# The second layer's input projection by one level of Strassen products, with values, gates and head outputs kept with tokens on partitions

## The chip, the cores and the metric

The kernel runs on one core of one Trainium2 chip. The metric is the device time of one execution in microseconds: the median of the runs, 807.87 us over three runs (806.84 to 807.95) for the kernel before. A profiled execution gives a trace of each engine: PE multiplies matrices, DVE (VectorE), ACT (ScalarE) and POOL (GpSimd) work on elements, SP issues most of the DMAs.

## The reference

Two pre-norm layers over 512 tokens of width 1024, then a last RMSNorm. Layer 1 (attention and pooling) stays as it is. Layer 2 is bidirectional retention with four heads; what the change touches is its input projection `h @ w_in`, whose columns are q, k (256 each for a head), v and gate (512 each for a head):

```python
def retention_layer(x, cos_r, sin_r, norm_g, w_in, decay_fwd, decay_bwd, gn_g, w_out):
    h = rms_norm(x, norm_g)
    q, k, v, gate = jnp.split(h @ w_in, [RET_QK, 2 * RET_QK, 2 * RET_QK + RET_V], axis=-1)
    q = apply_rope(q.reshape(B_, T, RET_HEADS, RET_DK), cos_r, sin_r)
    k = apply_rope(k.reshape(B_, T, RET_HEADS, RET_DK), cos_r, sin_r) * (RET_DK ** -0.5)
    o = retention(q, k, v)          # scores q k^T times a decay in |i - j|, times v, both directions
    o = group_norm(o) * gn_g        # over the 512 channels of a head
    return (o * jax.nn.silu(gate)) @ w_out
```

## The kernel before

Every fp32 product is made of three matmuls: each operand is split into a high part that PE takes whole and a remainder, and `mm3` (L71) issues high x high (L72), and the two mixed products (L75, L76). The split of a weight block of 128x1024 is `wsplit`: the high part is a cast on ACT (L108), the remainder a subtraction on DVE (L109); that of an activation is `split` (L81 on ACT, L82 on DVE). All work is handed to a tile framework that orders the instructions of each engine by itself as the program is built; only what `pin` names is held in program order. Each engine then runs its own list strictly in order, and waits for others by semaphores. SBUF tiles come from pools by tag (`BUFS`, L46), PSUM tiles from three tags: `mm` 4, `sc` 2, `tr` 2 banks.

In layer 2, x lies with channels on partitions (`xT`, eight chunks of 128 channels x 512 tokens). `close_layer` (L651) adds the last quarter of layer 1's output to a chunk (L652), scales it by the norm's gain and splits it (L655 on ACT, L656 on DVE). The token factor of the norm, r2, comes from Squares (L835), sums (L836), `token_sums` (L177), a power on POOL (L174, `pow_mhalf`) and `bcast` (L191), which spreads it over the partitions; it is applied behind the products, to the rope tables (L843, L844), the values (L714) and the gates (L743).

For each head the program computes q and k with channels on partitions (`qk_gemm`, four `gemm_T` blocks of 24 matmuls), rope (`rope_pair`, L690), the output projection of the head before (`r_out`, L770, 96 matmuls into the residual `acc`, which holds tokens on partitions), the decay table (`decay`, L660), the values with tokens on partitions (`r_values`, L700, 96 matmuls), the scores (`r_scores`, L724), the gates with channels on partitions (`r_gates`, L738, 96 matmuls), and the head's output with channels on partitions (`r_head_out`, L751). The residual is turned by 32 transposes (`acc_in`, L672) and copied out of PSUM on ACT (L682). After the last head, `finish` (L795) and `scale_out` (L814) do the last norm.

Of the kernel before, what the change touches and what calls it, by code (L numbers as in the profile page):

```python
# [12 lines left out]
F32R = mybir.dt.float32r  # L13
# [24 lines left out]
def trunk(ctx: ExitStack, tc: tile.TileContext, x, positions, a_norm_g, a_w_in, a_q_norm_g, a_w_uq,  # L38
# [7 lines left out]
    BUFS = {"hT": 16, "xT": 8, "y": 8, "V": 8, "qk": 8, "pt": 8, "t": 9, "l1": 13,   # L46
            "raw": 3, "wH": 4, "wL": 3, "sm": 24}
    PBUFS = {"mm": 4, "sc": 2, "tr": 2}

    def S(tag, shape=(P, T), dt=F32):  # L50
        count[0] += 1
        return sb.tile(list(shape), dt, tag=tag, name=f"{tag}_{count[0]}", bufs=BUFS[tag])

# [225 lines left out]
    posf = C("posf", (P, T))  # L279
# [123 lines left out]
    WB = 576  # L403
    plu = {}

    def pool_in(gi):
# [5 lines left out]
        def pool_ev(m, pt):  # L412
            u = S("pt", (P, WB))[:, :W]
# [4 lines left out]
            while step < w:  # L418
                nx = S("pt", (P, WB))[:, :W]
# [222 lines left out]
    idi = S("raw", (P, 1024), I32)[:, :E]  # L642
# [5 lines left out]
    h2H, h2L = [None] * 8, [None] * 8  # L648
    sqs = S("l1")

    def close_layer(m, pt):  # L651
        V.tensor_add(xT[m], pt, xT[m])  # L652
        h = S("hT", dt=F32R)
        l = S("hT", dt=F32R)
        act(h, xT[m], AF.Copy, scale=col(RN + m))  # L655
        V.scalar_tensor_tensor(out=l, in0=xT[m], scalar=col(RN + m), in1=f(h), op0=ALU.mult, op1=ALU.subtract)  # L656
        h2H[m], h2L[m] = h, l
# [9 lines left out]

    wr = r_w_in[0]
    wo = r_w_out[0]
    acc = [[None] * 2 for _ in range(4)]  # L670

    def acc_in(hf):  # L672
        pts = [PS(tag) for tag in ("tr", "tr", "sc", "sc")]
        for t in range(4):
            for k in range(4):
                nc.tensor.transpose(pts[t][:, k * P:(k + 1) * P], xT[hf * 4 + k][:, t * P:(t + 1) * P], ident)
        return pts

    def acc_set(hf, pts):
        for t in range(4):  # L680
            a = S("xT")
            nc.scalar.copy(a, pts[t])  # L682
            acc[t][hf] = a

    def qk_gemm(c0, n=2):
        pts = []
        gemm_T(wr, c0, n, lambda m, pt: pts.append(pt), h2H, h2L)
        return pts

    def rope_pair(pts):  # L690
        a, b, c, d = S("t"), S("t"), S("t"), S("t")
        V.tensor_mul(a, pts[0], cosr)
        V.tensor_mul(c, pts[0], sinr)
        V.tensor_mul(b, pts[1], sinr)
        V.tensor_mul(d, pts[1], cosr)
        V.tensor_sub(a, a, b)
        V.tensor_add(c, c, d)
        return split(a, "qk"), split(c, "qk")

    def r_values(h):  # L700
        pts = [PS("mm") for _ in range(4)]
        for kp in range(4):
            uH, uL = wunit(wr[kp * 256:(kp + 1) * 256, 2048 + h * T:2048 + (h + 1) * T]
                           .rearrange("(k p) n -> p k n", p=P), 2, T)
            for k2 in range(2):
                k = kp * 2 + k2
                for t in range(4):
                    tk = slice(t * P, (t + 1) * P)
                    mm3(pts[t], h2H[k][:, tk], h2L[k][:, tk], uH[:, k2], uL[:, k2], k == 0, k == 7)
        vH, vL = [], []  # L710
        for t in range(4):
            v = S("t")
            sm = S("sm", (P, 4))
            act(v, pts[t], AF.Copy, scale=r2[:, t:t + 1], accum_out=sm[:, 0:1])  # L714
# [5 lines left out]
            vH.append(hh)  # L720
            vL.append(ll)
        return vH, vL

    def r_scores(q, k, ds):  # L724
        sH, sL = [], []
        for j in range(4):
# [6 lines left out]
            a, b = split(s, "pt")  # L733
            sH.append(a)
            sL.append(b)
        return sH, sL

    def r_gates(h, m0=0, n=4):  # L738
        gs = []

        def ev(m, pt):
            t = S("t")
            V.tensor_mul(t, pt, R)  # L743
            g = S("l1")
            act(g, t, AF.Silu)
            gs.append(g)

        gemm_T(wr, 4096 + h * T + m0 * P, n, ev, h2H, h2L)
        return gs

    def r_head_out(h, vv, ss, gs, ytag):  # L751
        ys = []
        sq = None
        for m in range(4):
            ms = slice(m * P, (m + 1) * P)
            pt = PS("mm")
            for j in range(4):
                mm3(pt, vv[0][j][:, ms], vv[1][j][:, ms], ss[0][j], ss[1][j], j == 0, j == 3)
            t = S("t")
            act(t, pt, AF.Square)  # L760
            if sq is None:
                sq = t
            else:
                V.tensor_add(sq, sq, t)
            y = S("t")
            V.scalar_tensor_tensor(out=y, in0=pt, scalar=col(GN + h * 4 + m), in1=gs[m], op0=ALU.mult, op1=ALU.mult)
            ys.append(split(y, ytag))
        return ys, sq

    def r_out(h, ys, rs, last=False, mid=None):  # L770
        for hf in range(2):
            us = [wunit(wo[h * T + i * 256:h * T + (i + 1) * 256, hf * T:(hf + 1) * T]
                        .rearrange("(k p) n -> p k n", p=P), 2, T) for i in range(2)]
            for t in range(4):
                tk = slice(t * P, (t + 1) * P)
                n = 2 if last and hf == 1 and t == 3 else 1
                for c in range(n):
# [5 lines left out]
                    if mid and hf == 0 and t == 0:  # L783
# [42 lines left out]

    pend = None
    for h in range(4):
        if h == 0:
            pts = acc_in(0)  # L830
            pq = qk_gemm(0, 1)
            act(sqs, xT[0], AF.Square)
            for m in range(1, 8):
                t = S("t")
# [79 lines left out]
```

## Time and profile before

| | |
|---|---|
| median of three runs | 807.87 us (806.84 to 807.95) |
| the profiled execution | 807.98 us |
| its span (first to last instruction) | 806.2 us |
| mean granted PE clock | 0.997 |
| PE busy, DVE busy, ACT busy, POOL busy | 99%, 65%, 45%, 2% |

In the page and in the views of the trace, a row names the line of the kernel, the engine, the operation and its tiles, out<-in. A timeline row begins with the start in us from the span's start and the duration; a bracket behind a row is the engine's idle time before it and who released it. A window row gives the stretch, its length, and each engine's busy time with its count of instructions.

### The profile page before, as it was taken

The page shows a single profiled execution, that of the slowest core. Times are in us where ns is not written, and L with a number is a line of the kernel's source. Part 1 is how long each engine was busy: PE and PEld are TensorE (multiplying, and loading weights), DVE is VectorE, ACT ScalarE, POOL GpSimd, SP SyncE. Part 2 cuts the span into 40 slices and gives each one's busy share as a digit, 9 for nine tenths or more (in the row PEclk, how much of TensorE's full clock was granted, in tenths as well). Part 3 has the DMA queues.
Part 4 walks back from the last instruction along what each step waited for, and adds up shares of the span by engine and source line. Part 5 has one row for each costly group of instructions (what it writes and reads, how often), then busy time and mean ns, then how long its engine had stood idle before and what let it go on. Part 6 is the DMA issues. An engine that isn't in the chain of part 4 may idle for free.

```text
span 806.2 us, 9481 instructions
## 1 busy us (share of the span) xinstructions
PE 796.5 (99%) x3590; PEld 656.1 (81%) x3590; DVE 524.1 (65%) x895; ACT 364.4 (45%) x595; POOL 18.9 (2%) x45
## 2 busy tenths in 40 slices
PE   8999999999999999999999999999999999999996
PEld 6888888888888888888888888888888888888885
DVE  4689976767748687899564648363483535753655
ACT  6645346676627734328254522263232543253222
POOL 0010000000000000000000000000000000000003
PEclk9999999999999999999999999999999999999999
DMA  7523233221222212233323113323123221232112
GB/s 224 150 75 90 85 82 75 54 80 62 72 81 80 79 53 78 79 101 111 103 79 105 52 53 105 98 59 105 53 68 115 79 78 53 85 99 78 53 53 104
DMA packets 93589, 68.30 MB, mean 85 GB/s; under 512 B 7484, under 2 KB 83304, under 8 KB 93544
## 3 DMA queue, kind: packets, MB, share of 16 engines
q1 hardware_dynamic: 93240, 67.18, 28.4%
q8 instruction: 28, 0.46, 0.3%
q10 hardware_dynamic: 304, 0.53, 0.2%
q14 instruction: 17, 0.14, 0.1%
HBM read 64.29 MB, written 2.10 MB: 82 GB/s over the span
## 4 chain that ended last, share of the span: by engine, by line
PE 97%; DMA 1%; POOL 1%; issue 0%; SPq 0%; ACT 0%; DVE 0%; POOLq 0%
PE mm L72 29%; PE mm L75 29%; PE mm L76 29%; PE sc L72 2%; PE sc L76 2%; PE sc L75 2%; PE tr L560 2%; PE sc L541 1%; PE sc L542 1%; DMA l<-in_x_dram 1%; POOL t L820 0%; POOL sm L816 0%; PE tr L182 0%; PE mm L345 0%; PE mm L344 0%
## 5 line engine op out<-in xcount | busy, mean ns | idle before, releaser
L108 ACT CAST wH<-raw 128x1024 fp32r<-128x1024 f32 (+3 forms) x133 | 125.4, 946 | 291.2 <-PE mm L75 137.4
L109 DVE TENSOR_TENSOR wL<-raw,wH 128x1024 fp32r<-128x1024 f32 (+3 forms) x133 | 144.5, 1090 | 94.5 <-PE mm L76 42.1
L72 PE MATMUL mm<-hT,wH 128*128 128x512 f32 x480 | 187.9, 391 | 0.0
L75 PE MATMUL mm<-hT,wH 128*128 128x512 f32 x480 | 187.6, 391 | 0.0
L76 PE MATMUL mm<-hT,wL 128*128 128x512 f32 x480 | 187.6, 391 | 0.0
L76 PEld LDWEIGHTS mm<-hT,wL 128*128 128x128 f32 x480 | 90.6, 189 | 18.9
L75 PEld LDWEIGHTS mm<-hT,wH 128*128 128x128 f32 x480 | 90.4, 188 | 18.7
L72 PEld LDWEIGHTS mm<-hT,wH 128*128 128x128 f32 x480 | 90.5, 189 | 18.5
L75 PE MATMUL mm<-wL,hT 128*128 128x512 f32 (+1 forms) x164 | 63.0, 384 | 0.0
L72 PE MATMUL mm<-wH,hT 128*128 128x512 f32 (+1 forms) x164 | 62.9, 384 | 0.0
L76 PE MATMUL mm<-wH,hT 128*128 128x512 f32 (+1 forms) x164 | 62.8, 384 | 0.0
L786 DVE SCALAR_TENSOR_TENSOR xT<-mm,sm,xT 128x512 f32<-128x512 f32 (+1 forms) x33 | 24.2, 732 | 23.8 <-PE mm L76 23.8
L743 DVE TENSOR_TENSOR t<-mm,R 128x512 f32<-128x512 f32 x16 | 11.1, 691 | 43.2 <-PE mm L76 43.2
L75 PE MATMUL mm<-pt,V 128*128 128x512 f32 x96 | 37.8, 393 | 0.0
L72 PE MATMUL mm<-pt,V 128*128 128x512 f32 x96 | 37.5, 391 | 0.0
L76 PE MATMUL mm<-pt,V 128*128 128x512 f32 x96 | 37.5, 390 | 0.0
L75 PE MATMUL mm<-wL,y 128*128 128x512 f32 x96 | 37.4, 389 | 0.0
L72 PE MATMUL mm<-wH,y 128*128 128x512 f32 x96 | 37.4, 389 | 0.0
L76 PE MATMUL mm<-wH,y 128*128 128x512 f32 x96 | 37.3, 389 | 0.0
L75 PE MATMUL mm<-y,wH 128*128 128x512 f32 x96 | 37.2, 389 | 0.0
L76 PE MATMUL mm<-y,wL 128*128 128x512 f32 x96 | 37.2, 389 | 0.0
L72 PE MATMUL mm<-y,wH 128*128 128x512 f32 x96 | 37.2, 390 | 0.0
(238 smaller groups left out, 1329.8 us busy)
## 6 DMA issues: line engine op xcount, KB each, us to landing
raw<-in_r_w_in_dram SPq DMA_DIRECT2D x48, 512.0 KB, 3.8
raw<-in_a_w_in_dram SPq DMA_DIRECT2D x25, 512.0 KB, 3.9
raw<-in_a_w_out_dram SPq DMA_DIRECT2D x16, 512.0 KB, 3.5
raw<-in_r_w_out_dram SPq DMA_DIRECT2D x16, 512.0 KB, 3.4
l<-in_x_dram SPq DMA_DIRECT2D x8, 256.0 KB, 5.6
out_dram<-t SPq DMA_DIRECT2D x8, 256.0 KB, 2.0
raw<-in_a_w_in_dram SPq DMA_DIRECT2D x4, 384.0 KB, 4.1
raw<-in_a_w_uq_dram SPq DMA_DIRECT2D x8, 192.0 KB, 2.4
```

The source lines that it names most:

```text
L72: i = mm(pt, lhsT=lH, rhs=rH, start=st, stop=False)
L75: mm(pt, lhsT=lH, rhs=rL, start=False, stop=False)
L76: mm(pt, lhsT=lL, rhs=rH, start=False, stop=sp)
L108: then(nc.scalar.copy(h[:, c], raw[:, c]))
L109: then(V.tensor_sub(l[:, c], raw[:, c], f(h[:, c])))
L541: mm(pt, lhsT=st[:, tk], rhs=KH, start=False, stop=False)
L542: mm(pt, lhsT=st[:, tk], rhs=KL, start=False, stop=True)
L560: nc.tensor.transpose(pt[:, t * P:(t + 1) * P], es[t][:, j * P:(j + 1) * P], ident)
L743: V.tensor_mul(t, pt, R)
L786: V.scalar_tensor_tensor(out=a, in0=pt[:, :T // n], scalar=rs[:, t:t + 1], in1=a, op0=ALU.mult, op1=ALU.add)
```

## The change

The input projection of layer 2 is a 2x2 block product: the contraction is cut into even and odd 128-channel chunks, the tokens into two halves of 256, and the columns into two blocks, q and k of a head in `qk(h)`, gates and values of a head in `vg(h)`. `strassen` computes it with seven block products instead of eight (the form of Winograd): the activation forms A11, A12, A22, S1 to S4 are made once, at the end of layer 1, by `left_forms` on DVE and split (ACT, DVE); the weight sums are made for each head by POOL (`minus`), 12 of 128x1024 a head, and all weight blocks and sums are split as before. The parts of the result are gathered from three sets of PSUM banks (X, Y, Z) by `read`. In `qk` the 256 tokens of a half are the moving operand; in `vg` they are the stationary one, and 512 weight columns move.

Values, gates and head outputs now all have tokens on partitions. So the gate takes r2 as a per-partition scale of its Silu, the squares for the group norm are ACT's accumulators, and `turn` transposes the gated output back before `r_out`. Those accumulators replace `token_sums`; for r2 the Squares are taken of the turned residual (`residual`). The rope tables times R are kept as two pairs, CS and SC, one pair for each half of the tokens. The tiles that had tags of their own share one class of 72 buffers of 2 KB; `raw` has 6 buffers instead of 3, `tw` is new.

```diff
-    BUFS = {"hT": 16, "xT": 8, "y": 8, "V": 8, "qk": 8, "pt": 8, "t": 9, "l1": 13, 
-            "raw": 3, "wH": 4, "wL": 3, "sm": 24}
+    BUFS = {"b": 72, "raw": 6, "tw": 4, "wH": 4, "wL": 3, "sm": 24}
...
+    def left_forms(out, e, o, ge, go):
...
+        for src, g, a, b in ((e, ge, raw["A11"], a21), (o, go, raw["A12"], raw["A22"])):
+            V.tensor_scalar(out=a, in0=src[:, :H2], scalar1=g, scalar2=1.0, op0=ALU.mult, op1=ALU.mult)
+            V.tensor_scalar(out=b, in0=src[:, H2:], scalar1=g, scalar2=1.0, op0=ALU.mult, op1=ALU.mult)
+        V.tensor_add(raw["S1"], a21, raw["A22"])
+        V.tensor_sub(raw["S2"], raw["S1"], raw["A11"])
+        V.tensor_sub(raw["S3"], raw["A11"], a21)
+        V.tensor_sub(raw["S4"], raw["A12"], raw["S2"])
+        for z, names in ((z1, ("A11", "A12")), (z2, ("A22", "S1")), (z3, ("S2", "S3")), (z4, ("S4",))):
+            n = H2 * len(names)
+            h, l = S("hT", dt=F32R), S("hT", dt=F32R)
+            nc.scalar.copy(h[:, :n], z[:, :n])
+            V.tensor_sub(l[:, :n], z[:, :n], f(h[:, :n]))
...
+    def strassen(load, chunks, run, read):
...
+        product("A11", "X", b11, True)
+        t1 = [minus(b12[i], b11[i]) for i in rng]
+        product("S1", "Z", t1, True)
+        t2 = [minus(b22[i], t1[i]) for i in rng]
+        product("S2", "Y", t2, True)
+        b21 = [load(1, 0, i) for i in rng]
+        product("A12", "X", b21, False)
+        t4 = [minus(b21[i], t2[i]) for i in rng]
+        product("S3", "Y", [minus(b22[i], b12[i]) for i in rng], False)
+        product("S4", "Z", b22, False)
+        product("A22", "Y", t4, False)
...
     def close_layer(m, pt):
         V.tensor_add(xT[m], pt, xT[m])
-        h = S("hT", dt=F32R)
-        l = S("hT", dt=F32R)
-        act(h, xT[m], AF.Copy, scale=col(RN + m))
-        V.scalar_tensor_tensor(out=l, in0=xT[m], scalar=col(RN + m), in1=f(h), op0=ALU.mult, op1=ALU.subtract)
-        h2H[m], h2L[m] = h, l
+        if m % 2:
+            left_forms(forms[m // 2], xT[m - 1], xT[m], col(RN + m - 1), col(RN + m))
...
+    def residual():
...
+            for t in range(4):
+                a = S("xT")
+                nc.scalar.copy(a, pts[t])
+                acc[t][hf] = a
+                act(S("t"), a, AF.Square, accum_out=ss2[:, hf * 4 + t:hf * 4 + t + 1])
...
+    def qk(h):
...
+        def rope(n, half, c):
...
+            V.tensor_mul(m1, c, CS[half])
+            V.tensor_mul(m2, c, SC[half])
+            V.tensor_sub(outs[n][0][:, ts], m1[:, :H2], m1[:, H2:])
+            V.tensor_add(outs[n][1][:, ts], m2[:, :H2], m2[:, H2:])
...
+            if name == "A11":
+                got["p1"] = S("t")
+                nc.scalar.copy(got["p1"], X)
...
+            elif name == "A12":
+                rope("q", 0, X)
+            elif name == "S3":
+                c = got["v"]
+                V.tensor_add(c, Y, c)
+                rope("k", 1, c)
...
+    CS, SC = [S("cs"), S("cs")], [S("cs"), S("cs")]
+    for _ in residual():
+        pass
+    V.tensor_add(ss2[:, 0:4], ss2[:, 0:4], ss2[:, 4:8])
+    r2 = pow_mhalf(ss2[:, 0:4], 1.0 / DM)
+    rp = bcast(r2)
+    nc.scalar.copy(R, rp)
...
     for h in range(4):
...
+        q, k = qk(h)
+        if pend is not None:
+            yT = turn(h - 1, pend[0])
+            if h < 3:
+                r_out(h - 1, yT, pow_mhalf(pend[1], 1.0 / T))
         ds = decay(h)
...
+        ss = r_scores(q, k, ds)
+        vv, gs = vg(h)
+        last = pend
+        pend = r_head_out(ss, vv, gs)
```

What the framework's order makes of it is shown at three places. Lines of the kernel after are its own. The first is ACT's list at the boundary between the layers. Before (hT is the high part of a chunk of x, the xT copies are the residual, the last row is R):

```order
L655 ACTIVATE hT_810_3494<-xT_50_224,cols_63 128x512
L835 ACTIVATE t_833_3604<-xT_50_224 128x512
...
L682 COPY xT_836_3613<-tr_821_3540 128x512
L682 COPY xT_837_3615<-tr_822_3541 128x512
L682 COPY xT_838_3617<-sc_823_3542 128x512
L682 COPY xT_839_3619<-sc_824_3543 128x512
L81 CAST t_844_3652<-l1_784_3371 128x512
...
L207 ACTIVATE t_858_3705<-ident_101,sm_856_3702 128x128 x4
...
L842 COPY R_356<-tr_859_3714 128x512
```

After (the first row is the cast of the last activation form of the last pair; `t_901` in the last row is the first product of `qk(0)`):

```order
L675 CAST hT_851_3615<-t_844_3594 128x256
L751 COPY xT_862_3644<-tr_858_3624 128x512
...
L753 ACTIVATE t_863_3646,sm_853_3619<-xT_862_3644 128x512
...
L751 COPY xT_876_3684<-tr_871_3661 128x512
...
L753 ACTIVATE t_879_3690,sm_853_3619<-xT_878_3688 128x512
L751 COPY xT_880_3692<-sc_873_3663 128x512
L753 ACTIVATE t_881_3694,sm_853_3619<-xT_880_3692 128x512
L208 ACTIVATE t_887_3706<-ident_101,sm_885_3703 128x128 x4
L988 COPY R_356<-tr_888_3715 128x512
L791 COPY t_901_3768<-mm_889_3727 128x512
```

The residual's copies and Squares now follow one another behind the last form, and the copy of R and that of the first product stand behind all of them.

The second is PE's list in head 1, behind the products of q and k. Before (mm_1010 is the last block of k, mm_1025 the first of `r_out`):

```order
L75 MATMUL mm_1010_4387<-hT_820_3537,wH_1008_4383 128x512
L76 MATMUL mm_1010_4387<-hT_819_3536,wL_1009_4384 128x512
L72 MATMUL mm_1025_4442<-wH_1020_4432,y_963_4183 128x512
L75 MATMUL mm_1025_4442<-wL_1021_4433,y_963_4183 128x512
L76 MATMUL mm_1025_4442<-wH_1020_4432,y_964_4184 128x512
```

After (mm_1037 is the last product, tr are the transposes of `turn`, sc_1118 the first score tile, mm_1104 the first of `r_out`):

```order
L774 MATMUL mm_1037_4434<-hT_847_3607,wL_1073_4651 128x256
L916 MATMUL tr_1084_4701<-ident_101,l1_993_4220 128x128
...
L916 MATMUL tr_1087_4710<-ident_101,t_970_4102 128x128
L73 MATMUL sc_1118_4880<-qk_1076_4685,qk_1080_4693 128x512
L76 MATMUL sc_1118_4880<-qk_1077_4686,qk_1080_4693 128x512
L77 MATMUL sc_1118_4880<-qk_1076_4685,qk_1081_4694 128x512
L73 MATMUL mm_1104_4753<-wH_1099_4743,y_1085_4706 128x512
L916 MATMUL tr_1090_4719<-ident_101,l1_993_4220 128x128
...
L76 MATMUL mm_1104_4753<-wL_1100_4744,y_1085_4706 128x512
L77 MATMUL mm_1104_4753<-wH_1099_4743,y_1086_4707 128x512
```

The first three score matmuls, which read the split q and k, moved ahead of half of `turn` and of the whole of `r_out`.

The third is DVE's list at the same place, which makes those splits. Before:

```order
L694 TENSOR_TENSOR t_1012_4413<-mm_1010_4387,l1_755_3173 128x512
L695 TENSOR_TENSOR t_1014_4415<-mm_1010_4387,l1_754_3172 128x512
L696 TENSOR_TENSOR t_1011_4412<-t_1011_4412,t_1012_4413 128x512
L697 TENSOR_TENSOR t_1013_4414<-t_1013_4414,t_1014_4415 128x512
L786 SCALAR_TENSOR_TENSOR xT_836_3613<-mm_1025_4442,sm_998_4361,xT_836_3613 128x512
L82 TENSOR_TENSOR qk_1016_4423<-t_1011_4412,qk_1015_4422 128x512
L786 SCALAR_TENSOR_TENSOR xT_837_3615<-mm_1026_4456,sm_998_4361,xT_837_3615 128x512
L82 TENSOR_TENSOR qk_1018_4427<-t_1013_4414,qk_1017_4426 128x512
```

After (qc are the rotated halves, qk_1077 to qk_1083 the remainders of the split q and k):

```order
L810 TENSOR_TENSOR t_1048_4474<-mm_1037_4434,t_1048_4474 128x512
L110 TENSOR_TENSOR wL_1110_4812<-raw_1108_4809,wH_1109_4811 128x1024
L783 TENSOR_TENSOR t_1074_4679<-t_1048_4474,cs_855_3621 128x512
L784 TENSOR_TENSOR t_1075_4680<-t_1048_4474,cs_857_3623 128x512
L785 TENSOR_TENSOR qc_1039_4436<-t_1074_4679 128x256
L786 TENSOR_TENSOR qc_1040_4437<-t_1075_4680 128x256
L83 TENSOR_TENSOR qk_1077_4686<-qc_1039_4436,qk_1076_4685 128x512
L83 TENSOR_TENSOR qk_1079_4690<-qc_1040_4437,qk_1078_4689 128x512
L83 TENSOR_TENSOR qk_1081_4694<-qc_1041_4438,qk_1080_4693 128x512
L83 TENSOR_TENSOR qk_1083_4698<-qc_1042_4439,qk_1082_4697 128x512
```

The remainders of q and k, which alternated with the residual's additions of `r_out` (L786), now stand behind the last rope, with the weight remainders (L110) of `r_out` ahead of them.

More of the change, by code (lines that the diff above doesn't have):

```diff
@@ L665, in decay @@
         return [e[:, (3 - j) * P:(3 - j) * P + T] for j in range(4)]
-    wr = r_w_in[0]
+    wr = r_w_in[0].rearrange("(i two p) n -> p two i n", two=2, p=P)
     wo = r_w_out[0]
     acc = [[None] * 2 for _ in range(4)]
[L672 to L711, printed above, removed]
+    ss2 = S("sm", (P, 8))
```

250 lines of the change are left out of this document (168 added, 82 removed).

## The prediction

> **What bounds the kernel now.** I read the page's busy shares first, then its chain of waits.
>
> ```profile
> PE 796.5 (99%) x3590; PEld 656.1 (81%) x3590; DVE 524.1 (65%) x895; ACT 364.4 (45%) x595; POOL 18.9 (2%) x45
> PE 97%; DMA 1%; POOL 1%; issue 0%; SPq 0%; ACT 0%; DVE 0%; POOLq 0%
> ```
>
> PE is busy for 99% of the 806.2 us span and holds 97% of the chain that ended last. So every microsecond of PE work that goes is a microsecond gained, as long as PE goes on without waiting. Whether it does depends on the slack of the engines that feed it; that is the second reading, the busy times by stage (columns after the window: its length, then PE, PEld, DVE, ACT, POOL).
>
> ```profile
> 357.20:379.00 21.80, 21.80 (x98) 17.98 (x97) 20.64 (x30) 15.98 (x23) 0.00 (x0) 1.00 0.39 114
> 463.00:567.00 104.00, 104.00 (x459) 85.83 (x459) 55.90 (x84) 37.70 (x53) 1.01 (x1) 1.00 0.28 81
> ```
>
> In one whole retention head (463 to 567) DVE works 55.90 of 104 us, so on average there is room. In the last stage of layer 1 (357.20 to 379.00, the quarter of w_out that `close_layer` closes) DVE already works 20.64 of 21.80 us: there is none. The change puts work on DVE in both. The third reading is the pace of PE and of the others, from the timelines (start, duration; the step from one start to the next is the pace).
>
> ```profile
> 784.80 0.39 PE L76 MATMUL mm<-wH,hT 128*128 128x512 f32 x1
> ...
> 796.36 0.39 PE L76 MATMUL mm<-wH,hT 128*128 128x512 f32 x1
> 796.59 0.28 PE L72 MATMUL mm<-wH,hT 128*128 128x256 f32 x1
> 796.70 0.28 PE L75 MATMUL mm<-wL,hT 128*128 128x256 f32 x1
> ...
> 799.34 0.28 PE L76 MATMUL mm<-wH,hT 128*128 128x256 f32 x1
> ```
>
> From 784.80 to 796.36 there are 51 steps: 0.2267 us for a matmul of 512 columns. From 796.70 to 799.34 there are 22: 0.120 us for 256 columns, 6% more per column than the wide one.
>
> ```profile
> 378.98 1.03 PE L676 MATMUL tr<-ident,xT 128*128 128x128 f32 x8
> 379.86 1.04 PE L676 MATMUL sc<-ident,xT 128*128 128x128 f32 x8
> 380.65 0.48 PE L72 MATMUL mm<-hT,wH 128*128 128x512 f32 x1
> ```
>
> Sixteen transposes take 1.67 us, 0.104 each.
>
> **The change part by part.**
>
> *PE work.* A head's q and k cost 96 wide matmuls before (21.8 us) and 7 products of 24 narrow ones now (168 x 0.120 = 20.2 us). Its values and gates cost 192 wide ones before, 7 x 24 = 168 wide ones now. So of the one eighth that Strassen saves, the narrow pace eats most in q and k. Over four heads: 384 + 96 wide ones go, 672 narrow ones come, the five pairs of token sums (10 wide ones) go, and `turn` brings 64 transposes: -490 x 0.2267 + 672 x 0.120 + 64 x 0.104 = -111.1 + 80.6 + 6.7 = **-23.7 us** of PE work. That is all that the change can gain.
>
> *Prices of the feeding engines.*
>
> ```profile
> 379.79 0.68 DVE L836 TENSOR_TENSOR l<-l,t 128x512 f32<-128x512 f32 x1
> 380.39 1.22 DVE L109 TENSOR_TENSOR wL<-raw,wH 128x1024 fp32r<-128x1024 f32 x1
> 381.52 0.75 DVE L656 SCALAR_TENSOR_TENSOR hT<-xT,cols,hT 128x512 fp32r<-128x512 f32 x1
> 382.19 0.68 DVE L836 TENSOR_TENSOR l<-l,t 128x512 f32<-128x512 f32 x1
> ```
>
> ```profile
> 379.00 1.05 ACT L108 CAST wH<-raw 128x1024 fp32r<-128x1024 f32 x1
> 379.95 0.72 ACT L655 ACTIVATE hT<-xT,cols 128x512 fp32r<-128x512 f32 x1
> 380.57 0.61 ACT L835 ACTIVATE t<-xT 128x512 f32<-128x512 f32 x1
> 381.10 1.05 ACT L682 COPY xT<-tr 128x512 f32<-128x512 f32 x2
> 382.04 1.08 ACT L682 COPY xT<-sc 128x512 f32<-128x512 f32 x2
> ```
>
> Back to back, DVE takes 0.60 us for a 512-wide two-input operation, 1.13 for a 1024-wide one and 0.67 for L656. From 0.60 and 1.13 I estimate 0.33 for a 256-wide one. ACT takes 0.95 for a weight cast, 0.47 for a copy out of PSUM, 0.62 for L655, 0.53 for a Square; for a Square whose accumulator is read I take 0.65, a little over L655.
>
> *The layer boundary.* Count from the start of the last quarter of w_out (357.2 before). Each pair of x chunks now takes 4 scalings (at about 0.3), 4 additions of 256 and the splits, 3 x 0.60 + 0.33: 4.65 us on DVE, four pairs 18.6, where L656 goes (8 x 0.67 = 5.4). DVE's 20.64 us become 33.9, and the quarter ends at 21.8: the last form of the last pair is there at about 34. The earliest possible, if other DVE work stood back, is 21.8 + 0.6 + 4.65 = 27. In ACT's rows (quoted with the change) all eight residual copies and eight Squares stand behind the cast of that last form, with three weight casts: 8 x (0.47 + 0.65) + 3 x 0.95 = 11.8 us, so the last Square ends at about 46. Only then comes the chain to R:
>
> ```profile
> 393.99 0.17 DVE L172 TENSOR_SCALAR sm<-sm 128x4 f32<-128x4 f32 x1
> 394.24 1.02 POOL L174 TENSOR_TENSOR sm<-sm,mhalf 128x4 f32<-128x4 f32 x1 [57.47 <-DVE sm L172]
> 395.29 0.17 DVE L198 CAST sm<-sm 128x4 fp32r<-128x4 f32 x1 [1.14 <-POOL sm L174]
> 395.58 0.87 DVE L205 TENSOR_SCALAR t<-ident,sm 128x128 fp32r<-128x128 f32 x4
> 395.70 1.28 ACT L207 ACTIVATE t<-ident,sm 128x128 fp32r<-128x128 f32 x4 [3.00 <-DVE sm L200]
> 397.54 1.05 ACT L108 CAST wH<-raw 128x1024 fp32r<-128x1024 f32 x1 [0.56 <-ACT t L207]
> 398.49 0.57 ACT L842 COPY R<-tr 128x512 f32<-128x512 f32 x1
> ```
>
> From 393.99 to 399.06 is 5.07 us, 4.1 without the weight cast that stood in it. With 0.2 for the sum of the squares and 0.5 for the copy of the first product (behind R in ACT's rows, and A12's first matmul writes into the bank that it reads) PE can begin product A12 at 46.4 + 0.2 + 4.1 + 0.5 = 51. Before that PE has 21.8 + 32 x 0.104 + 72 x 0.120 + 0.5 = 34.2 us of work: it waits **17 us** where it waited for nothing. With the forms ready at 27 the wait is 10; that is the lower end. Before, nothing queued behind R but rope, and qk's matmuls (L72) hid the chain.
>
> *GpSimd beside DVE.* 48 subtractions of 128x1024 are new on POOL, 12 a head, and no row shows one. The nearest rows on POOL and the one place where POOL and a two-input DVE operation overlap:
>
> ```profile
> 335.84 0.93 POOL L644 CAST l<-raw 128x896 int16<-128x896 int32 x1
> ...
> 793.84 1.37 POOL L820 TENSOR_SCALAR t<-t,sm 128x512 f32<-128x512 f32 x2
> ```
>
> ```profile
> 789.42 0.69 DVE L803 TENSOR_TENSOR t<-xT,l 128x512 f32<-128x512 f32 x1
> ...
> 794.86 0.89 DVE L803 TENSOR_TENSOR t<-xT,l 128x512 f32<-128x512 f32 x1
> ```
>
> One input of 896 takes 0.93, so 1024 take 1.06; two passes give 2.1. I take 2.1, as there are two inputs. The DVE operation that started at 794.86 under the POOL pair (793.84 to 795.21) ended at 795.75, 0.54 after it: it waited until POOL was done, and its own work took about its last 0.54. So a subtraction costs DVE between nothing and 2.1 us each time that DVE has two SBUF inputs to read. At the boundary four of them fall into the DVE stretch: 0 to 8.4 us on top of the 17. Three more stand ahead of the power in POOL's queue. I take +3: **20 us**, between 10 and 26. The Trainium skill ("GPSIMD Engine Reference", section 3.1 on elementwise cycle accounting) has 4497 ns for an fp32 tensor_tensor of 2048 elements; halved, an estimate of 2.25 us for one of these. By that price the four would take 9.0 instead of 8.4 us and the upper end would rise by 0.6; no run here shows the operation yet.
>
> *Heads 1 and 2.* q and k of head h run from t = 0 to 20.2, and A12 ends at 4 x 2.88 = 11.5. After that DVE has, in its row order, 4 rope halves (2 x 0.60 + 2 x 0.33 = 1.86), 4 weight remainders (1.13), 3 reads (0.60) and 3 splits (0.60) up to the k remainder: 7.4 + 4.5 + 1.8 + 1.8 = 15.5, so it is done at 27. PE, after A22 and eight transposes (0.83), stands at 21.0 before score matmuls that need that split, and the rest of `turn` and the whole of `r_out`, which need nothing of it, stand behind them. PE waits 6, and about 1 more for the evacuation of the transposes in DVE's queue behind the splits: 7 a head; 11 when two of the next head's POOL subtractions block DVE in that time, 5 if DVE is ahead. I take **9 each, 18**. Before, the 96 matmuls of `r_out` (21.8 us) and those of the values lay between rope and the scores, and the same splits were hidden.
>
> *Heads 0 and 3.* In head 0 the scores stand inside the second chunk of vg's product S1 and wait 1.5 (unblocked) to 5.5: **3**. In head 3, 36 vg matmuls (8.2 us) stand ahead of the rest and cover most: 0 to 4, **2**.
>
> *Smaller terms.* At the start the last load of x is queued behind two weight loads more on SP, and the Squares of L323 come later on ACT; both are covered by the first projection or not: 0 to 5, **1**. In vg a head has 168 x 0.2267 = 38 us on PE, and on DVE 14 remainders (15.8), ten sums (6.0), four score and four value operations (8 x 0.67) and four splits (2.4), 30 together: I cost it at nothing, hidden by those matmuls; without that cover DVE's 30 would be the bound, still below 38. r_w_in is loaded with the same 48 transfers.
>
> *The clock.* PE's first matmuls:
>
> ```profile
> 9.38 0.59 PE L75 MATMUL mm<-hT,wH 128*128 128x512 f32 x1
> ...
> 12.32 0.63 PE L76 MATMUL mm<-hT,wL 128*128 128x512 f32 x1
> 12.75 0.43 PE L72 MATMUL mm<-hT,wH 128*128 128x512 f32 x1
> ```
>
> Eight matmuls start from 9.38 to 12.75, 0.42 us each instead of 0.2267: 1.6 us lost at the start. Whether it is lost again after a long wait no row shows, as PE never waits: 0 to 1.6 for each of three long gaps, 0 to 5, **2**. The Trainium skill ("TensorE: Matmul & The Clock Gate", Part 1) says that the clock is halved again after an idle window of about 3.4 us and that warming takes as long, which speaks for the upper end, 5, and the sum would be 3 higher by it; the start rows agree with its halved rate.
>
> *Sum.* 806.2 - 23.7 + 20 + 18 + 3 + 2 + 1 + 2 = 828.5 us of span. The profiled run took 807.98, 1.8 beyond its span, and lies within 0.1 of the median of 807.87: **830 us**.
>
> **The rivals.**
> 1. *PE's saving comes through.* DVE and ACT keep up, since the scheduler's rows bind less than I read. Then 806.2 - 23.7 + 1.8 = 784 us, up to 796 with 12 us of waits. For it: DVE's average slack (55.90 of 104). Against it: the 20.64 of 21.80 at the boundary. It decides if the forms' last cast is there by 24 instead of 34. Faster. Chance 0.14.
> 2. *Only the boundary waits*; the heads' splits are in time. 806.2 - 23.7 + 17 + 3 + 2 + 1.8 = 806, between 802 and 812: about even. Chance 0.09.
> 3. *POOL blocks DVE everywhere and the clock falls after each gap.* Boundary 26, heads 22, head 0 5.5, head 3 4, start 1, clock 5: 806.2 - 23.7 + 63.5 + 1.8 = 848. It decides once a subtraction takes 2.1 or more and blocks each time. The other side of rival 1: slower. Chance 0.15.
> 4. *The change doesn't save what it says.* If the narrow matmul went at 0.135 because its weight load were not hidden, q and k would cost more than before (22.7 against 21.8 a head) and 10 us come on top of the forecast: 840. Against it: 22 narrow steps, each with its own weights, at 0.120. Within the forecast's range.
>
> **How the numbers follow.** Forecast 0.62, from 815 (boundary 12, heads 6 each) to 842. Rivals 1, 2 and 3 hold 0.14, 0.09 and 0.15. A measurement of this kernel tells about 0.2% (1.6 us) from no change. Faster: 0.14 and a third of rival 2, 0.17; same: another third, 0.03; slower: 0.80. The range leaves out rival 1 below (0.14) and the upper part of rival 3 (0.05): 803 to 848.
>
> **What would show it.** In the profile after: PE's busy matmul time lower by 23.7 us over the span, narrow ones 0.120 apart; a gap of 10 to 26 us on PE at the first A12 matmul (L772), released by ACT's copy at L791 or L988; gaps of 5 to 11 us at the first score matmul (L73) of heads 1 and 2, released by DVE's splits (L83); POOL's L702 at about 2.1 us and DVE operations of L697 with 1.22 lengthened where they overlap it; slower matmuls behind each gap. I am wrong if PE stays at 99%, if the boundary gap is under 5 us, or if the time is under 803.

## The result, and the profile after

The changed kernel takes **915.5 us**, the median of four runs (913.9 to 917.2); the kernel before took 807.9 beside it (four runs, 806.8 to 809.2). The ratio of the times is 1.133, with a 95% interval from 1.130 to 1.136: 109 us slower over the profiled spans (915.2 against 806.2), where 22 had been forecast. The page of the kernel after has these lines, in the order busy shares, granted clock in 40 slices, and chain that ended last:

```profile
PE 817.5 (89%) x3836; PEld 673.0 (74%) x3836; DVE 661.3 (72%) x974; ACT 414.0 (45%) x670; POOL 163.1 (18%) x93
PEclk9899999898999999997689998899897999999999
PE 64%; DVE 22%; ACT 5%; issue 3%; DMA 1%; SPq 0%; POOL 0%; POOLq 0%; DVEq 0%; ACTq 0%
```

PE is no longer the whole chain: 22% of it is DVE's. And although matmul work was taken out, PE's busy time rose by 21 us, since part of it ran at a lower clock. Where this happens is read from the windows, before and after, cut at the start of the last quarter of w_out and at its end (columns: window, its length, then PE, PEld, DVE, ACT, POOL busy with their counts, granted clock, DMA share, GB/s). Before:

```profile
0.00:357.22 357.22, 354.09 (x1615) 290.07 (x1615) 269.01 (x496) 188.98 (x335) 7.23 (x30) 1.00 0.31 89
378.98:806.20 427.22, 420.64 (x1881) 348.08 (x1879) 234.54 (x371) 159.46 (x239) 11.69 (x15) 1.00 0.26 80
```

After, with layer 2 cut further at the first A12 product (460.29) and at the heads:

```profile
0.00:395.35 395.35, 364.63 (x1614) 297.52 (x1615) 270.82 (x491) 190.97 (x335) 12.04 (x31) 0.97 0.29 84
395.35:418.99 23.64, 22.78 (x97) 17.66 (x96) 23.57 (x32) 9.44 (x12) 7.61 (x4) 1.00 0.31 93
418.99:460.29 41.30, 21.42 (x108) 17.88 (x106) 29.39 (x56) 21.91 (x46) 8.81 (x4) 0.64 0.12 36
460.29:540.33 80.04, 72.64 (x336) 59.17 (x337) 66.18 (x81) 38.77 (x54) 32.35 (x9) 0.95 0.21 66
540.33:660.03 119.70, 106.02 (x522) 88.01 (x520) 88.13 (x95) 48.55 (x67) 33.49 (x13) 0.91 0.22 71
660.03:780.17 120.14, 104.77 (x522) 87.18 (x520) 89.19 (x95) 48.55 (x67) 38.35 (x15) 0.93 0.22 71
780.17:862.99 82.82, 79.39 (x425) 67.40 (x424) 64.23 (x81) 41.42 (x60) 22.78 (x7) 0.98 0.25 77
862.99:915.20 52.21, 45.84 (x221) 38.14 (x219) 29.82 (x47) 14.37 (x29) 7.64 (x11) 0.97 0.14 51
```

The first row is the surprise: layer 1, whose code hardly changed, is 38.1 us longer. The length of a window less PE's busy time is PE's idle time; so the 109 us split into

| | PE work | PE slower per matmul | PE idle | sum |
|---|---|---|---|---|
| layer 1 up to the last quarter | 0 | +10.5 | +27.6 | +38.1 |
| the last quarter | 0 | +1.0 | +0.9 | +1.9 |
| layer 2 | -23.7 | +33.2 | +59.5 | +69.0 |

For layer 2, -23.7 is the forecast work, and "slower" is what PE's busy time (430.1 over its rows) has beyond 420.6 - 23.7. Not all of it is a lower pace: a matmul of 512 columns is busy for 0.39 us where the next one starts after 0.2267, so the last one before each of some 50 waits adds about 0.16, by this estimate 8 of the 44.7 us.

What released PE is in the waits view (waiting group, who it waited for, us in all, times, longest):

```profile
PE sc L73 <- ACT qk L82: 19.3, 3, 9.5
PE mm L73 <- ACT pt L82: 18.5, 3, 7.0
PE tr L210 <- DVE t L206: 10.1, 3, 8.8
PE mm L73 <- ACT V L846: 5.7, 6, 1.2
PE mm L773 <- DVE hT L676: 4.4, 4, 2.7
PE mm L772 <- ACT hT L675: 4.3, 4, 2.6
PE mm L73 <- DVE V L83: 3.7, 1, 3.7
```

Rows 1 and 4 are layer 2's heads (scores wait for the split q and k, the head's output for the values); rows 3 (but for 1.2 us), 5 and 6 are the boundary; rows 2 and 7 are layer 1.

**Layer 1.** The second of its three waits of row 2, with ACT's, DVE's and SP's rows from the timeline (start, duration; a bracket is the engine's idle time and its releaser):

```profile
154.82 2.48 SPq L355 DMA_DIRECT2D t<-t  x4
...
159.81 0.69 DVE L357 TENSOR_TENSOR t<-t,l 128x512 f32<-128x512 f32 x1 [2.80 <-DMA t<-t]
160.53 0.69 DVE L358 TENSOR_TENSOR t<-t,t 128x512 f32<-128x512 f32 x1
161.31 0.62 ACT L514 CAST l<-t 64x512 fp32r<-64x512 f32 x1 [6.18 <-DVE t L358]
161.96 0.61 ACT L516 CAST l<-t 64x512 fp32r<-64x512 f32 x1
162.60 1.07 ACT L82 CAST pt<-tr 128x512 fp32r<-128x512 f32 x2
163.24 0.80 PE L73 MATMUL mm<-pt,V 128*128 128x512 f32 x1 [7.03 <-ACT pt L82]
```

The rope of q (`rope_rows`) swaps rows by four small DMAs; ACT stood 6.18 us before the cast that needs them, and the casts of the softmax, which PE was waiting for, stood behind it. Before, the four casts of that block (L81 there) stood ahead of it:

```profile
141.25 0.59 ACT L81 CAST pt<-tr 128x512 fp32r<-128x512 f32 x1
...
142.14 0.60 ACT L81 CAST pt<-tr 128x512 fp32r<-128x512 f32 x1
143.60 0.58 ACT L81 CAST pt<-tr 128x512 fp32r<-128x512 f32 x1 [0.87 <-PE tr L560]
...
146.18 0.57 ACT L81 CAST pt<-tr 128x512 fp32r<-128x512 f32 x1
...
149.51 0.60 ACT L514 CAST l<-t 64x512 fp32r<-64x512 f32 x1
```

The same instructions, in another order.

**A head.** In head 1, POOL's subtractions and DVE's row beside them, and PE's score matmul that waits for the end of it:

```profile
560.75 7.08 POOL L702 TENSOR_TENSOR tw<-raw,raw 128x1024 f32<-128x1024 f32 x2 [17.44 <-DMA raw<-in_r_w_in_dram]
561.00 0.68 DVE L784 TENSOR_TENSOR t<-t,cs 128x512 f32<-128x512 f32 x1
...
562.87 2.77 DVE L110 TENSOR_TENSOR wL<-raw,wH 128x1024 fp32r<-128x1024 f32 x1
565.56 2.82 DVE L783 TENSOR_TENSOR t<-t,cs 128x512 f32<-128x512 f32 x1
...
570.00 4.22 DVE L83 TENSOR_TENSOR qk<-qc,qk 128x512 fp32r<-128x512 f32 x4 [0.35 <-ACT qk L82]
571.07 0.80 PE L73 MATMUL sc<-qk,qk 128*128 128x512 f32 x1 [9.54 <-ACT qk L82]
```

L110 takes 2.77 instead of 1.22 and L783 2.82 instead of 0.69, on the chain that PE waits for.

### The profile page after: what moved, and what is told of

It is laid out like the page before. It is cut to its first block, busy times and chain, and to the rows that moved or that the text cites. A ratio compares the mean times of both kernels' runs of the same rounds, so it can differ in the third digit from the quotient of the medians.

```text
span 915.2 us, 10268 instructions
## 1 busy us (share of the span) xinstructions
PE 817.5 (89%) x3836; PEld 673.0 (74%) x3836; DVE 661.3 (72%) x974; ACT 414.0 (45%) x670; POOL 163.1 (18%) x93
## 4 chain that ended last, share of the span: by engine, by line
PE 64%; DVE 22%; ACT 5%; issue 3%; DMA 1%; SPq 0%; POOL 0%; POOLq 0%; DVEq 0%; ACTq 0%
PE mm L73 14%; PE mm L76 13%; PE mm L77 13%; DVE wL L697 5%; DVE wL L110 3%; PE mm L832 2%; PE mm L833 2%; PE mm L831 2%; PE mm L773 2%; PE mm L772 2%; PE mm L774 2%; PE tr L560 2%; DVE t L783 2%; DVE V L847 1%; PE sc L77 1%
## 5 line engine op out<-in xcount | busy, mean ns | idle before, releaser
L702 POOL TENSOR_TENSOR tw<-raw,tw 128x1024 f32<-128x1024 f32 x24 | 75.8, 3163 | 155.9 <-DVE wL L697 55.9
L110 DVE TENSOR_TENSOR wL<-raw,wH 128x1024 fp32r<-128x1024 f32 (+3 forms) x85 | 95.2, 1125 | 9.6 <-issue 4.3
L73 PE MATMUL mm<-hT,wH 128*128 128x512 f32 x224 | 87.8, 392 | 0.0
L76 PE MATMUL mm<-hT,wH 128*128 128x512 f32 x224 | 87.3, 390 | 0.0
L77 PE MATMUL mm<-hT,wL 128*128 128x512 f32 x224 | 87.3, 390 | 0.0
L702 POOL TENSOR_TENSOR tw<-raw,raw 128x1024 f32<-128x1024 f32 x24 | 66.5, 2775 | 109.4 <-DMA raw<-in_r_w_in_dram 54.5
L772 PE MATMUL mm<-hT,wH 128*128 128x256 f32 x224 | 67.3, 300 | 5.5 <-ACT hT L675 4.3
L773 PE MATMUL mm<-hT,wH 128*128 128x256 f32 x224 | 67.1, 299 | 4.4 <-DVE hT L676 4.4
L697 DVE TENSOR_TENSOR wL<-tw,wH 128x1024 fp32r<-128x1024 f32 x48 | 67.7, 1414 | 3.1 <-PE mm L774 1.7
L774 PE MATMUL mm<-hT,wL 128*128 128x256 f32 x224 | 66.5, 297 | 1.1 <-DVE wL L697 1.1
L831 PE MATMUL mm<-wH,hT 128*128 128x512 f32 x144 | 56.8, 394 | 0.0
L833 PE MATMUL mm<-wH,hT 128*128 128x512 f32 x144 | 56.4, 392 | 0.0
L772 PEld LDWEIGHTS mm<-hT,wH 128*128 128x128 f32 x224 | 45.8, 205 | 7.3 <-ACT hT L675 5.5
L73 PE MATMUL mm<-wH,y 128*128 128x512 f32 (+1 forms) x132 | 51.2, 388 | 0.0
L77 PE MATMUL mm<-wH,y 128*128 128x512 f32 (+1 forms) x132 | 51.0, 386 | 0.0
```

The lines of the kernel that those rows point to most:

```text
L73: i = mm(pt, lhsT=lH, rhs=rH, start=st, stop=False)
L76: mm(pt, lhsT=lH, rhs=rL, start=False, stop=False)
L77: mm(pt, lhsT=lL, rhs=rH, start=False, stop=sp)
L110: then(V.tensor_sub(l[:, c], raw[:, c], f(h[:, c])))
L697: V.tensor_sub(l, w, f(h))
L702: G.tensor_sub(t, a, b)
```

## The experiments

Times are device us; the kernel before, run with each group, took 806.7 to 808.2. One run each, except where an interval is given.

**The class of tiles alone.** The kernel before, with only the shared class, `raw` of 6, `tw`, and the scratch tiles that moved to them; no Strassen products.

```diff
-    BUFS = {"hT": 16, "xT": 8, "y": 8, "V": 8, "qk": 8, "pt": 8, "t": 9, "l1": 13, 
-            "raw": 3, "wH": 4, "wL": 3, "sm": 24}
+    BUFS = {"b": 72, "raw": 6, "tw": 4, "wH": 4, "wL": 3, "sm": 24}
...
+        home = tag if tag in BUFS else "b"
```

> The kernel before with the one class of 72 buffers, raw 6 and tw 4 alone, no Strassen. Theory (the shared class lets the scheduler reorder layer 1, and PE waits there): the last quarter of w_out starts near 395 us instead of 357, and the time is 838 to 852 us. Rival (layer 1 is late because of what Strassen adds, weight blocks loaded early for example): the quarter starts at 357 and the time stays at 805 to 812 us.

845.2. Layer 1 ends 36.4 us later (393.58), layer 2 takes 427.8 as before (427.2). PE's waits are the ones seen in the kernel after:

```profile
PE mm L72 <- ACT pt L81: 18.6, 3, 6.7
PE mm L72 <- DVE V L82: 3.7, 1, 3.7
```

So the class, with the six weight buffers and `tw`, reorders layer 1 without any Strassen product and costs nearly all that layer 1 lost. Which of the three does it was not tried apart.

**The weight sums: without them, and on DVE.** In the first, `minus` returns its first operand and the sums are left out of the computation; in the second, DVE makes them.

```diff
         def minus(a, b):
-            t = S("tw", (P, 1024))
-            G.tensor_sub(t, a, b)
-            return t
+            return a
```

> The changed kernel without the 48 subtractions on GpSimd: each product takes the first block in place of the difference, which leaves out the weight sums. Theory (GpSimd holds up DVE's two-input operations, 59 us of lengthened DVE operations in layer 2, some half of it on the path): L697's mean falls from 1.42 and 1.71 to 1.13 to 1.25, heads 1 and 2 shrink by 6 to 10 us each, the time is 870 to 895 us. Rival (DVE's own queue is too long, blocking or not): 908 to 916 us.

858.6 without them, below both ranges: 57 us hang on them.

```diff
-            G.tensor_sub(t, a, b)
+            V.tensor_sub(t, a, b)
```

> The changed kernel with the 48 subtractions on DVE instead of GpSimd. Theory (a subtraction on GpSimd costs DVE about as much as doing it): 48 x 1.13 = 54 us more for DVE against 59 us less of lengthened operations, 900 to 925 us. Rival (GpSimd's work is nearly free, DVE's length is the bound): 940 to 970 us.

879.6 on DVE, below both ranges too: 36 us faster than on POOL, although 48 x 1.13 = 54 us of work came to the engine that heads wait for. The remainders of the split weights show why (groups of DVE's instructions: busy us, mean ns, idle before). After:

```profile
L697 DVE TENSOR_TENSOR wL<-tw,wH 128x1024 fp32r<-128x1024 f32 x48 | 67.7, 1414 | 3.1 <-PE mm L774 1.7 <-PE sc L832 0.5 <-PE mm L832 0.3
L697 DVE TENSOR_TENSOR wL<-raw,wH 128x1024 fp32r<-128x1024 f32 x36 | 61.0, 1697 | 12.1 <-PE mm L774 7.8 <-PE sc L832 1.5 <-PE mm L76 1.3
```

With the sums on DVE:

```profile
L697 DVE TENSOR_TENSOR wL<-tw,wH 128x1024 fp32r<-128x1024 f32 x48 | 58.6, 1222 | 4.4 <-PE sc L832 1.5 <-PE mm L774 1.4 <-PE mm L832 0.8
L697 DVE TENSOR_TENSOR wL<-raw,wH 128x1024 fp32r<-128x1024 f32 x36 | 44.0, 1221 | 12.2 <-PE mm L774 6.5 <-PE sc L832 2.9 <-PE mm L832 1.6
```

The mean falls to 1.22 us, the undisturbed value: the 1.41 and 1.70 were blocking. With both kernels the wait for the split q and k falls to 5.8 us at its longest, from 9.5, as the working without blocking had it (6 and about 1 more).

**The scores' place.** The scores are called behind the values instead of ahead of them.

```diff
-        ss = r_scores(q, k, ds)
         vv, gs = vg(h)
+        ss = r_scores(q, k, ds)
```

> The changed kernel with the scores asked for behind the values and gates, as before the change. Theory (PE waits for the split q and k only because three score matmuls stand ahead of turn and r_out): the gaps of 9.5 us in heads 1 and 2 go with 3 us of half clock behind each, and some 4 in head 0: 883 to 897 us. Rival (the wait only moves, to the splits of the transposed outputs or to the weight remainders in vg): 908 to 918 us.

915.2: no change. The wait only moved: 10.7 us at `r_out` for the transposed outputs, and up to 5.1 at the scores:

```profile
PE mm L73 <- ACT y L919: 21.3, 2, 10.7
...
PE sc L73 <- DVE t L876: 13.2, 4, 5.1
```

PE waits for DVE's list at this place, and moving the scores alone only changes which block meets the wait.

**Layer 1's order by hand.** After, with the Squares of the norm pinned behind each load, and values and softmax casts called ahead of the rope.

```diff
+        for t in range(4):
+            junk = S("t")
+            pin(act(junk[:, 0:256], xt[t][q], AF.Square, accum_out=ssq[:, 4 * t + q:4 * t + q + 1]))
...
+    vv = values(0)
     kq = rope_rows(kr, CA, SA)
...
+        prev = (probs_T(es), vv, h % 4, gp[:, h % 2])
         if h % 2 == 0 and h < 6:
             nst = q_rope(h // 2 + 1)
```

> The changed kernel with three places of layer 1 written in another order: the first Squares pinned behind each pair's transposes, values ahead of the rotated key, and the rotated query of the next pair behind the transposed probabilities. Theory (in layer 1 PE waits because casts and subtractions that wait for rope's transfer stand ahead of those that PE needs): the waits of 7.0, 6.3, 5.2, 3.7 and 2.5 us go with some 2 us of half clock behind each: the last quarter of w_out starts at 362 to 372 us instead of 395 and the time is 880 to 893 us. Rival (the reordering is spread over all of layer 1): 905 to 916 us.

902.6: a miss, between the two ranges. The last quarter starts at 380.86 instead of 395.35, 14.5 of the 38 us; new waits took the place of the old ones (4.0 for the softmax in `PE tr L559 <- DVE t L550`). Moving three blocks does not undo a reordering of the whole layer.

**Turn early.** `turn` and the power for the head before are called inside `qk`, behind its second product.

```diff
-        q, k = qk(h)
-        if pend is not None:
-            yT = turn(h - 1, pend[0])
...
+            q, k = qk(h, lambda: tt.extend((turn(h - 1, pend[0]), pow_mhalf(pend[1], 1.0 / T))), "S1")
```

> The changed kernel with turn asked for behind the second product of q and k, so that r_out can follow the products without a wait and covers rope and the splits. Theory (PE waits in heads 1 and 2 since everything that it could do stands behind DVE's rope and splits): 10.6 us of wait and 3 of half clock go in each of two heads, 885 to 893 us. Rival (the wait moves on, as with the scores asked for late): 908 to 918 us.

897.0, 18.6 less. `r_out` now stands ready while DVE finishes rope, and the 9.5 us waits at the scores are gone; smaller ones came for the weight remainders (7.5 us in two, for DVE's L110). Less than expected.

**The norm's chain behind the third product.** Residual, r2 and the tables CS, SC are called inside `qk(0)`.

```diff
+        if h == 0:
+            q, k = qk(0, norm2)
```

> The changed kernel with the residual's transposes, copies, Squares and the chain to R asked for behind the third product of head 0's q and k. Theory (A12 waits for ACT's sixteen residual operations and the chain to R): A12 starts 25 to 32 us behind the quarter's end instead of 41, and half clock is shorter: 897 to 907 us. Rival (the forms on DVE are what is late): 911 to 916 us.

910.9, at the lower end of the rival. A12 does start 28.0 us behind the end of the quarter (445.13 against 417.13), as the theory had it, but little of this is kept. The 8.8 us wait at `bcast` (L210) went down to 2.5, but the forms bind all the same: 4.7 and 4.6 us at L773 and L772, as in the kernel after, and a new 5.5 for a weight remainder.

**All four together** (layer 1's order, turn early, norm late, sums on DVE).

> The three orders together with the subtractions on DVE. Theory (Strassen's 23.7 us are there, and waits and half clock took them): the waits fall to 10 to 25 us, 794 to 810 us. Rival (DVE's length is the bound in layer 2 whatever the order): 820 to 850 us.

837.0 (ratio 1.036, 1.033 to 1.039): far better, yet above the expectation, mostly because layer 1 was not mended: its last quarter still starts at 382.73. Layer 2 from its end on takes 431.2, four over before, with heads of 98.3 us (from first product to first product, 508.58 to 606.94).

**Two pools.** After, with layer 1's tags and buffers as they were, and one class of 53 buffers opened for layer 2 only, before the last quarter; layer 2's `qk` tiles move to the tag `V`.

```diff
+    OLD = {"hT": 16, "y": 8, "qk": 8, "pt": 8, "t": 9, "l1": 13, "raw": 3}
+    NEW = {"b": 53, "raw": 6, "tw": 4}
...
+    first.close()
+    part.append(ctx.enter_context(tc.tile_pool(name="two", bufs=1)))
     w_out_quarter(3, ys2, close_layer)
```

> The changed kernel with the one class undone for layer 1: layer 1 has its own tiles by tag and three weight blocks, as before, and the shared class of layer 2 takes their place when it ends. PE's order in layer 1 is then the old one. Theory (the class and the early weight blocks cost layer 1 its 38 us): the last quarter of w_out starts at 357 to 359 us and the time is 875 to 882 us. Rival (part of the 38 us is made up later, since layer 2 then gets its weights later): 885 to 916 us.

868.2, 47 us less. Layer 1 is PE's old order again, and the last quarter starts at 362.38 instead of 395.35: 33.0 us. Another 17.4 us come from layer 2 (478.8 instead of 496.2), whose order changed as well: the 9.5 us waits at the scores are gone, and `turn` waits for DVE's remainders instead (second row). So not all of the 47 us is layer 1. The first row is new too: the first weight cast of the last quarter needs a buffer of the class that has just been opened in the old one's place.

```profile
PE mm L84 <- ACT wH L120: 5.8, 1, 5.8
PE tr L929 <- DVE y L933: 20.0, 6, 7.2
```

**Two pools and the other three edits** (turn early, norm late, sums on DVE).

> The same, with turn early, the norm late and the subtractions on DVE, that is all four causes taken away at once except the forms themselves. Theory: 837 less the 25 us that layer 1 still lost, 806 to 815 us, with what is left in the 20 us between the quarter's end and the scores of head 0, where DVE makes the forms. Rival (with layer 1 earlier the heads wait again): 820 to 837 us.

816.1, one above what was expected.

**The scalings of the forms on ACT, and the first decay table ahead of the boundary.**

```diff
-            V.tensor_scalar(out=a, in0=src[:, :H2], scalar1=g, scalar2=1.0, op0=ALU.mult, op1=ALU.mult)
-            V.tensor_scalar(out=b, in0=src[:, H2:], scalar1=g, scalar2=1.0, op0=ALU.mult, op1=ALU.mult)
+            act(a, src[:, :H2], AF.Copy, scale=g)
+            act(b, src[:, H2:], AF.Copy, scale=g)
```

> The same, with the forms' 16 scalings on ACT and head 0's decay table ahead of the boundary, to shorten DVE's work between the layers. Theory (DVE's forms bind there, 8 us a pair against 5.4 of PE): 4 to 8 us less than the kernel without these two, 799 to 809 us. Rival (the chain by way of ACT is longer, so nothing is won): 0 to 3 us less.

811.8 (ratio 1.0053, 1.0037 to 1.0070): 4.3 less than the one run before it, inside the 4 to 8 expected, though not under 809. The 5.8 us wait at the pool's opening was still there.

**That wait removed.** The weight buffers `raw` stay in the pool of both layers; half of the blocks are loaded into four buffers of their own (`raw2`), b22 - b12 overwrites b12, and `tw` has three buffers. The diff shows the pools alone.

```diff
-    BUFS = {"xT": 8, "V": 8, "l0": 3, "wH": 4, "wL": 3, "sm": 24}
-    OLD = {"hT": 16, "y": 8, "qk": 8, "pt": 8, "t": 9, "l1": 13, "raw": 3}
-    NEW = {"b": 53, "raw": 6, "tw": 4}
+    BUFS = {"xT": 8, "V": 8, "l0": 3, "raw": 3, "wH": 4, "wL": 3, "sm": 24}
+    OLD = {"hT": 16, "y": 8, "qk": 8, "pt": 8, "t": 9, "l1": 13}
+    NEW = {"b": 53, "raw2": 4, "tw": 3}
```

> The best version so far, with the three buffers of the weights (raw) kept in the class that both layers share, so that the last quarter of w_out no longer waits for layer 1's pool to be given back; the Strassen blocks get four buffers of their own beside them (raw2), b22 - b12 is written over b12, and the differences have three buffers instead of four. Theory (the remaining 4 us over the kernel before are the wait of 5.82 us at the pool switch): the wait goes, and the time falls from 811.8 to 803 to 808, at or below that of before. Rival (the forms on DVE, or the fewer buffers of the blocks, take up what the wait gives back): 809 to 815, with waits for forms or for weight casts in the place of the 5.82 us.

**805.9**, the median of 12 runs (803.3 to 807.1), against 807.7 for the kernel before (17 runs): ratio 0.9975, 0.9965 to 0.9985. The theory held, and this version is faster than both kernels, by a quarter of a per cent. Its windows:

```profile
0.00:356.90 356.90, 353.27 (x1614) 289.36 (x1615) 269.07 (x496) 189.11 (x335) 7.26 (x30) 1.00 0.32 89
356.90:378.70 21.80, 21.80 (x97) 18.03 (x97) 20.97 (x34) 14.06 (x23) 0.00 (x0) 1.00 0.58 195
378.70:804.10 425.40, 407.49 (x2127) 348.17 (x2125) 344.99 (x478) 215.01 (x329) 12.57 (x15) 0.98 0.24 76
```

Layer 1 and the last quarter are as before, and layer 2 takes 425.4 instead of 427.2. Of the 23.7 us of work saved, 11.3 are still lost to idle time (17.9 instead of 6.6) and 10.6 to slower matmuls (407.5 against 420.6 - 23.7 = 396.9); the waits that remain are short ones, at the boundary and in head 0, and 1.0 us in head 3.

## Why the prediction was right or wrong

The direction was right, the size was not: 915.5 lies far above the range. Layer 1 came to 38.1 us where the sum had 1. In layer 2 the idle time grew by 59.5 where the terms for waits make 43 (20 + 18 + 3 + 2), and slower matmuls took 33.2 where it had 2. By the prediction's own terms:

- **PE's work, -23.7: held.** PE has 246 matmuls more (3590 to 3836), as -490 + 672 + 64 has it. Undisturbed, a head takes 98.3 us from first product to first product, in the version with all four edits and in the last one; before, it took 103.95 (465.09 to 569.04). That is 5.65 less for each of four heads, 22.6 of the 23.7.
- **"At the start ... both are covered by the first projection or not: 0 to 5, 1": the step that failed.** I priced the class of tiles by what it does to the first loads, and took the rest of layer 1 as unchanged. The class with its weight buffers cost 37.0 us (845.2 against 808.2), and with layer 1's tags given back its last quarter starts 33.0 us earlier. The runs show that a rule of buffers is a rule of order under this framework: in one in-order list a cast that waits for a DMA came ahead of casts that PE waited for. That it orders by which buffer comes free is my explanation and was not tried by itself. The rows of order that the prediction rested on were those around the Strassen products; none was of layer 1.
- **The clock, "0 to 5, 2": the second failure.** I counted three restarts of 1.6 us. The slower matmuls add up to 44.7 us in the table above (10.5, 1.0, 33.2, of which some 8 are the ends of matmuls before waits), and in the rows behind the waits it is the pace of the start, 0.43 a matmul. Many waits restart it, those of layer 1 and those of the values too, and the row in the section on the hardware puts some 3 us on one such stretch. Between the quarter and A12 alone, 21.4 us of PE time stand for 12.4 of work (34.2 - 21.8): 9 us, at a granted clock of 0.64.
- **The boundary's wait, 20: the working held to 3 us, the 3 for POOL in it did not.** PE's idle time between the end of the quarter and A12 is 41.30 - 21.42 = 19.9 us, but that it meets the 20 is luck. A12 starts 64.9 us behind the start of the quarter (460.29 - 395.35), where the working had 51, or 54 with POOL's 3. The forms are late; the last casts of them, after and in `no_sums`:

```profile
438.13 1.45 ACT L675 CAST hT<-t 128x512 fp32r<-128x512 f32 x3 [0.31 <-DVE t L668]
422.20 1.45 ACT L675 CAST hT<-t 128x512 fp32r<-128x512 f32 x3 [0.31 <-DVE t L668]
```

They end 44.2 us behind the start of the quarter, and without the subtractions 32.9 (it starts at 390.75 there), with A12 at 54.0; I had 34 and 51. So POOL's work beside DVE cost about 11 us here, where I took 3 and at most 8.4: DVE operations between 393.65 and 429.42 take 10 us longer than they do alone. PE meets this in two places, where I had put the whole wait at one: 9.8 us at the forms and a weight remainder, and 10 at the chain to R (8.8 at `bcast`, 1.2 at ACT's copy at L791, which releases A12 as forecast). Taking the chain away in `norm_late` gave only 4.6 us, since the forms then bound.
- **Heads 1 and 2, 9 each: mechanism right, too small.** They last 119.7 and 120.1 us, 21.6 more than the work; 13.7 and 15.4 of it are idle time, the rest slower matmuls. The wait at the scores was 9.5, until ACT's casts of the split (L82) behind DVE's rope, and about 1 more in two short gaps for DVE's remainders (L83): 10.6 for the forecast 7 to 11. Missing were the waits for the values in the head's output (about 2 us in each head, L846), which I had costed at nothing under the matmuls of vg, and the slow matmuls behind both.
- **Heads 0 and 3, 3 and 2: about right** for the waits at the place named (2.8 before L831 for DVE's L891 in head 0; 1.8 in head 3).
- **The subtractions, 2.1 us each, blocking between nothing and 2.1: the upper end.** Undisturbed, one takes 2.40 us, 0.3 more than I had, and DVE operations beside one came out up to 2.1 longer. The Trainium skill ("GPSIMD Engine Reference", section 3.1) leads to an estimate of 2.25, which the trace puts 7% higher. The 57 us that go with them (`no_sums`) are more than the terms of the forecast held for it.
- **Rivals.** The third (blocking everywhere, clock down after each gap, 848) named the mechanism of layer 2, at too low a price; the first two fell. The fourth, a slower pace of the narrow matmuls, fell too: 98.3 us a head leave no room for it.

What the four parts cost is shown by taking each away, but they do not add: the pools (47, of it 17 in layer 2), the sums on DVE (36), turn (19) and the norm (5) make 107, and all of them together gave 99 (816.1). Shown is that the class with its weight buffers costs layer 1's part, that POOL's blocking lengthens DVE's list, and that this list is what heads wait for; how much of layer 2's loss is the clock's alone was not tried by itself.

## What to carry to other kernels

Under a framework that orders the instructions itself, a change of pools or tags can change the order everywhere: compare every engine's list over the whole program, not only around the new code. An engine at 99% has saved work to gain only as long as the one that feeds it has slack in that stage; here DVE had none at the boundary, and the waits were paid twice, in idle time and, many of them, in slow matmuls behind it. A second elementwise engine is no free helper: moving 54 us of work back to the busy DVE was 36 us faster than leaving it on POOL.

## What the hardware showed that was not expected

**Short waits lower the clock.** At the output of head 1 no wait was longer than 1.23 us, and the matmuls behind it still ran slow (PE's timeline):

```profile
642.85 0.39 PE L833 MATMUL sc<-wH,hT 128*128 128x512 f32 x1
643.93 0.50 PE L73 MATMUL mm<-V,pt 128*128 128x512 f32 x1 [0.70 <-ACT V L846]
644.72 0.50 PE L76 MATMUL mm<-V,pt 128*128 128x512 f32 x1 [0.28 <-DVE V L847]
...
646.67 0.79 PE L73 MATMUL mm<-V,pt 128*128 128x512 f32 x1 [1.23 <-ACT V L846]
...
648.48 0.63 PE L73 MATMUL mm<-V,pt 128*128 128x512 f32 x1
...
652.32 0.60 PE L73 MATMUL mm<-V,pt 128*128 128x512 f32 x1
...
652.99 0.40 PE L77 MATMUL mm<-V,pt 128*128 128x512 f32 x1
```

From 648.48 to 652.32 there are nine steps of 0.427 us, against 0.2267 at full pace; from 646.67 to 652.32 some 3 us are lost, more than the waits' own 2.2. The Trainium skill ("TensorE: Matmul & The Clock Gate", "A second HAM failure mode: psum-queue depth-cycling") describes such swings of the clock from frequent small idle times in another kernel, which agrees; by the idle window of about 3.4 us that its Part 1 states, taken alone, this row would not have been slowed.

**POOL and DVE.** A two-input DVE operation beside a subtraction on POOL took 2.77 and 2.82 us where 1.22 and 0.69 are usual, and two subtractions took 7.08 where 4.80 would be twice the undisturbed time: each held up the other. The Trainium skill ("SBUF — State Buffer", "Who interferes with whom") says that a DVE instruction with two SBUF inputs contends with a GpSimd instruction that reads SBUF, and that the order of issue decides who blocks; the lengths above agree with that, in both directions. At the boundary a scaling with one tile as its input (L666 at 429.42) took 2.43 us beside a subtraction, and 0.34 without.
